# A hybrid decoder layer on one core: modulation in four column groups, two projections half ahead, and a first stage in written order

## The chip, the cores and the metric

The kernel runs on one core of a Trainium2 chip. A core has five engines with queues of their own: TensorE (PE in the profile; its weight loads are PEld), VectorE (DVE), ScalarE (ACT), GpSimd (POOL) and SyncE (SP), which here only issues transfers. Each engine works through its queue in order; semaphores tie the queues together. The metric is the device time of the program in microseconds, as the median of several executions.

## The reference

The reference computes one step of a hybrid decoder layer for a prompt (1024 rows) and eight single rows (the samples), with the same weights. The lines that matter here are those of the projection and of the compression; kv has six kinds (0 to 5), of which the even ones are rotated:

```python
    mod = jax.nn.silu(c) @ p['w_ada'] + p['b_ada']
    shift, scale, gate = jnp.split(mod[:, None, :], 3, axis=-1)
    h = rmsnorm(x, p['g_pre']) * (1 + scale) + shift
    z = h @ p['w_in']
...
    q = rope(zq.reshape(B, T, N_HEADS, HEAD_DIM), pos).reshape(B, T, KV_HEADS, HEADS_PER_GROUP, HEAD_DIM)
    kv = zkv.reshape(B, T, 6, KV_HEADS, HEAD_DIM)
    kv = jnp.stack([rope(kv[:, :, i], pos) if i % 2 == 0 else kv[:, :, i] for i in range(6)], axis=2)
...
    kc = compress(kv[:, :, 0], p['pe_cmp'][0], p['w_cmp1'][0], p['w_cmp2'][0])
    vc = compress(kv[:, :, 1], p['pe_cmp'][1], p['w_cmp1'][1], p['w_cmp2'][1])
```

Behind it come attention in three branches, a gated short convolution, and an output projection with a norm. The condition c has nine rows, one for the prompt and one for each sample.

## The kernel before

Activations stand transposed: model columns on partitions (eight tiles of 128, index k or f), the 1032 rows along the free side in three chunks c of 344 (`CH`). A product in near-fp32 precision is made of three fp32r products: each operand is split into a high part (a rounded copy, on ACT or DVE) and a low part (the difference, on DVE or POOL), and high·high, high·low and low·high are added up. `mm` (line 102), `copy` (lines 106 and 108) and `sub` (line 111) are helpers through which nearly all of that goes, so the lines of the profile are often theirs.

**The first stage** turns x into `Hh` and `Hl`, the split h. For each tile t of 128 rows, `norm_x(t)` squares and sums on ACT (`sq`), makes the mean on DVE (`ss`) and the inverse root on POOL; `scale_x(t)` multiplies on DVE; `trans_x(t)` transposes eight blocks on PE into two banks `psS`, which DVE and ACT copy into `xT`. The modulation has six blocks of 512 columns of `w_ada`; four are needed here: 2 and 3 are the scale for f = 0..3 and 4..7, 0 and 1 the shift. `ada(b)` multiplies the nine condition rows with a block (tiles `ar`, eight of 128 x 512): even k as an fp32 product (`cf`), odd k split into `ah` and `al` with two products (`cA`). `ada_end(b)` copies the sum to `mod`, adds the bias row b_ada that was loaded into its last row, and turns it by four small products with `ksel`; the result becomes `mA` or `mB`. `make_h(f, c)` is one ACT instruction (scale `mA`, bias `mB`) into `htmp`, a cast into `Hh` and a subtraction into `Hl`.

**Weights** of the projections come through the class `Weights`: `load` fetches a piece into one of three buffers `wraw`, `do_split` splits it into `wh` and `wl` (three buffers each), `release` frees one and splits the next. The first pieces are the K/V kinds 0 and 1 (two halves of K each), then q. A projection has 72 products, 24 a chunk.

**Behind the stage** the first projection (kind 0) runs half by half of K, then `proj` does kind 1 and q 0, q 1, with small jobs hung in at given places: `rows_out` and `x_prompt` (of kind 0), and `x_sample`, which needs rows of the paged cache. These are fetched by sixteen indirect transfers on POOL (`gather`, line 417) by the table `idx`, which DVE makes from the page table. `compress1(0)` needs all of them.

**Order.** A scheduler orders each engine's queue from the written program by its own estimates; buffers (`bufs=`) tie transfers and work: four tiles of x, eight `ar`, one `mod`.

Of the kernel before, what the change touches and what calls it, by code (L numbers as in the profile page):

```python
# [39 lines left out]
def constants():  # L40
# [41 lines left out]
def _build(ctx, tc, nc, I, O):  # L82
# [36 lines left out]
    prmT = cst.tile([128, 52], F32, name="prmT")  # L119
# [86 lines left out]
    W.add_cols(kvc(0))  # L206
    W.add_cols(kvc(1))
# [74 lines left out]


    xT = sp.tile([128, KT, TT], F32, name="xT")
    pt = bank("T")
    for k in range(KT):
        PE.transpose(pt[:, k * 9:(k + 1) * 9], ct[:, k * 128:(k + 1) * 128], ident[:9, :9])
    cf = sp.tile([128, KT, 18], F32, name="cf")
    V.memset(cf, 0.0)
    th = sp.tile([128, KT, 9], F32, name="th")  # L290
    cT = pt[:, 0:72].rearrange("p (k c) -> p k c", c=9)
    A.activation(th, cT, AF.Tanh, scale=0.5)
    V.scalar_tensor_tensor(th, th, 1.0, cT, op0=OP.add, op1=OP.mult)
    V.tensor_scalar(cf[:, :, 0:9], th, 0.5, None, op0=OP.mult)
    copy(V, cA[:, :, 0:9], cf[:, :, 0:9])
    sub(V, cA[:, :, 9:18], cf[:, :, 0:9], cA[:, :, 0:9])
# [66 lines left out]
    def make_h(f, c):  # L363
# [11 lines left out]
    load_x(0)
    load_x(1)
    load_x(2)
    load_x(3)
# [1 line left out]
    load_params()  # L380
    load_x(4)
    load_x(5)
    load_x(6)
    load_x(7)
    load_x(8)
# [25 lines left out]
    cache = I["cache_kv_pages"][0]  # L411
    rows2 = cache.rearrange("n p (h k) g d -> (n p h) (k g d)", h=2)

    def gather(out, s, what):

        for par in range(2):
            nc.gpsimd.indirect_dma_start(
                out=out[:, par], out_offset=None, in_=rows2,
                in_offset=bass.IndirectOffsetOnAxis(ap=idx[:, what, s, par:par + 1], axis=0))
# [4 lines left out]
    norm_x(0)  # L424
    scale_x(0)
    trans_x(0)
    norm_x(1)
    scale_x(1)
    trans_x(1)
    norm_x(2)  # L430
    scale_x(2)
    trans_x(2)
    norm_x(3)
    scale_x(3)
    trans_x(3)
    ada(2)
    pt = bank("T")
    PE.transpose(pt[:, 0:52], prm, ident[:52, :52])
    copy(V, prmT, pt[:, 0:52])
    V.tensor_scalar(prmT[:, 8:20], prmT[:, 8:20], 0.5, None, op0=OP.mult)  # L440
    norm_x(4)
    scale_x(4)
    trans_x(4)
    norm_x(5)
    scale_x(5)
    trans_x(5)
    norm_x(6)
    scale_x(6)
    trans_x(6)
    norm_x(7)  # L450
    scale_x(7)
    trans_x(7)
    norm_x(8)
    scale_x(8)
    trans_x(8)
    ada(0)
    scale_done(2, ada_end(2))
    copy(V, mB[:, 0:4, :], ada_end(0))
    make_h(0, 0)
    make_h(1, 0)  # L460
    make_h(2, 0)
    make_h(3, 0)
    W.do_split()
    ada(3)
    W.do_split()
    ada(1)
    make_h(0, 1)
    make_h(1, 1)
    make_h(2, 1)
    make_h(3, 1)  # L470
    make_h(0, 2)
    make_h(1, 2)
    make_h(2, 2)
    make_h(3, 2)
    scale_done(3, ada_end(3))
    copy(V, mB[:, 4:8, :], ada_end(1))
# [938 lines left out]
```

## Time and profile before

| | us |
|---|---|
| median of 3 runs | 1108.38 (1108.06 to 1109.43) |
| profiled execution, own time | 1110.11 |
| its span, first to last instruction | 1108.3 |
| PE busy | 1068.2 |
| DVE busy | 679.4 |
| ACT busy | 458.2 |
| POOL busy | 148.6 |

The profile is of one execution; its time is the span and 1.8 us around it. PE's busy time is nearly the span, but matmul ends are modelled, so stalls are better read from the timeline of a stretch: each row gives the start, the busy time, engine, line, operation, output and inputs, and in brackets the idle time before it with what ended it.

### The profile page before, as it was taken

To read this page: it belongs to the slowest core of one execution; us is meant where nothing else is said; L and a number is where in the kernel's file an instruction comes from. 1 tells how busy PE (TensorE), PEld (TensorE's weight loads), DVE (VectorE), ACT (ScalarE), POOL (GpSimd) and SP (SyncE) were. 2 spreads that over 40 slices of the span, in tenths; PEclk is the share of its full clock that TensorE was granted. 3 is DMA by queue.
4 is the path that set the end of the run, shared out by engine and by line. 5 is a ranking of instruction groups with operands and counts; after the bars stand their busy time and mean duration, and the time that the engine had idled before them with its cause. 6 is when DMAs were issued, how large, how long until landed. Compare 5 with 4: busy or idle time off the path is not lost.

```text
span 1108.3 us, 17275 instructions
## 1 busy us (share of the span) xinstructions
PE 1068.2 (96%) x6406; PEld 970.8 (88%) x6406; DVE 679.4 (61%) x1819; ACT 458.2 (41%) x1025; POOL 148.6 (13%) x190
## 2 busy tenths in 40 slices
PE   6989999999999999999999999999999999999997
PEld 3288999988888899888888999999999999998785
DVE  5865567546988898878987844434356321484433
ACT  5647353446677767776665311111012111121220
POOL 2233000012232111111111510000000000020000
PEclk9889999998999999999999999999999999999999
DMA  9634322310000000000000322362232112242222
GB/s 326 182 80 129 99 74 56 92 40 20 20 20 20 20 20 13 12 16 20 20 20 20 92 65 57 96 190 58 58 96 49 47 43 53 86 124 78 67 87 76
DMA packets 97122, 75.97 MB, mean 69 GB/s; under 512 B 24775, under 2 KB 81270, under 8 KB 97038
## 3 DMA queue, kind: packets, MB, share of 16 engines
q1 hardware_dynamic: 95494, 70.67, 22.6%
q0 software_dynamic: 1536, 4.20, 1.2%
q8 instruction: 50, 0.82, 0.3%
q14 instruction: 34, 0.28, 0.1%
q10 hardware_dynamic: 8, 0.01, 0.0%
HBM read 65.84 MB, written 9.01 MB: 68 GB/s over the span
## 4 chain that ended last, share of the span: by engine, by line
PE 82%; DVE 11%; ACT 3%; DMA 2%; issue 1%; POOL 0%; DVEq 0%; POOLq 0%; SPq 0%; ACTq 0%
PE psacc L102 50%; PE psS L102 17%; PE psO L102 6%; PE psT L987 5%; DVE P L955 3%; DVE P L939 2%; ACT P L942 1%; PE psT L102 1%; PE psS L360 1%; DVE pl L111 1%; DVE pc L111 1%; DVE qh L108 1%; DMA mod<-b_ada 1%; DVE sm L948 1%; DMA ar<-w_ada 1%
## 5 line engine op out<-in xcount | busy, mean ns | idle before, releaser
L102 PE MATMUL psacc<-Hh,wh 128*128 128x344 f32 x1096 | 363.6, 332 | 0.0
L102 PE MATMUL psacc<-Hh,wl 128*128 128x344 f32 x1096 | 352.4, 322 | 0.0
L102 PE MATMUL psacc<-Hl,wh 128*128 128x344 f32 x1096 | 352.2, 322 | 0.0
L102 PEld LDWEIGHTS psacc<-Hh,wh 128*128 128x128 f32 x1096 | 207.5, 189 | 6.1 <-issue 0.4
L102 PEld LDWEIGHTS psacc<-Hl,wh 128*128 128x128 f32 x1096 | 207.6, 189 | 4.5 <-issue 0.4
L102 PEld LDWEIGHTS psacc<-Hh,wl 128*128 128x128 f32 x1096 | 206.9, 189 | 2.2 <-DVE wl L111 0.5
L942 ACT ACTIVATE P<-P,mx 128x64 f32<-128x64 f32 (+8 forms) x192 | 115.0, 600 | 48.4 <-DVE mx L939 47.8
L108 DVE CAST wh<-wraw 128x512 fp32r<-128x512 f32 x78 | 34.1, 442 | 120.3 <-PE psacc L102 114.1
L111 DVE TENSOR_TENSOR pl<-psT,ph 128x512 fp32r<-128x512 f32 x132 | 89.7, 686 | 28.5 <-ACT ph L106 27.9
L111 DVE TENSOR_TENSOR wl<-wraw,wh 128x512 fp32r<-128x512 f32 x114 | 77.9, 687 | 30.1 <-ACT wh L106 25.4
L106 ACT ACTIVATE ph<-psT 128x512 fp32r<-128x512 f32 x132 | 77.5, 591 | 39.5 <-PE psT L987 38.8
L939 DVE CUSTOM_DVE_ANT_0 P<-psS,kbig 128x64 f32<-128x64 f32 (+4 forms) x192 | 81.1, 433 | 11.4 <-PE psS L102 10.5
L987 PE MATMUL psT<-ident,P 128*128 128x128 f32 x528 | 83.8, 277 | 2.7 <-DVE mx L939 1.4
L987 PEld LDWEIGHTS psT<-ident,P 128*128 128x128 f32 x528 | 64.3, 142 | 13.6 <-issue 3.5
L102 PE MATMUL psS<-K,qh 128*128 128x384 f32 (+3 forms) x192 | 66.1, 347 | 2.1 <-DVE mx L939 1.6
L111 POOL TENSOR_TENSOR wl<-wraw,wh 128x512 fp32r<-128x512 f32 x26 | 34.6, 1333 | 224.9 <-ACT wh L106 207.3
L102 PE MATMUL psS<-K,ql 128*128 128x384 f32 (+3 forms) x192 | 63.7, 333 | 0.0
L102 PE MATMUL psO<-pl,V 128*128 128x512 f32 x132 | 60.1, 456 | 1.0 <-DVE pl L111 0.9
L106 ACT ACTIVATE wh<-wraw 128x512 fp32r<-128x512 f32 x62 | 38.8, 627 | 41.4 <-PE psS L102 20.2
L111 POOL TENSOR_TENSOR WOl<-wor,WOh 128x512 fp32r<-128x512 f32 x8 | 11.4, 1419 | 328.4 <-PE psS L102 303.7
L102 PE MATMUL psO<-ph,V 128*128 128x512 f32 x132 | 52.1, 395 | 0.0
L955 DVE TENSOR_SCALAR P<-P,sm 128x640 f32<-128x640 f32 (+7 forms) x104 | 47.2, 512 | 0.7
(346 smaller groups left out, 1839.1 us busy)
## 6 DMA issues: line engine op xcount, KB each, us to landing
wraw<-w_in SPq DMA_DIRECT2D x76, 256.0 KB
ar<-w_ada SPq DMA_DIRECT2D x32, 256.0 KB
x<-x_prompt SPq DMA_DIRECT2D x8, 512.0 KB
wraw<-w_in SPq DMA_DIRECT2D x32, 128.0 KB
wraw<-w_cmp SPq DMA_DIRECT2D x16, 256.0 KB
wraw<-w_ada SPq DMA_DIRECT2D x16, 256.0 KB
wor<-w_out SPq DMA_DIRECT2D x16, 256.0 KB
xr<-x_prompt SPq DMA_DIRECT2D x8, 512.0 KB
```

Source lines behind the costliest of these rows:

```text
L102: PE.matmul(out, lhsT, rhs, start=start, stop=stop, skip_group_check=True)
L106: A.activation(out, in_, AF.Copy)
L108: eng.tensor_copy(out, in_)
L111: eng.tensor_tensor(out=out, in0=a, in1=b, op=OP.subtract)
L360: PE.transpose(pt[:, f * 128:(f + 1) * 128], xs[t][:, (4 * h + f) * 128:(4 * h + f + 1) * 128], ident)
L939: V.tensor_tensor_reduce(out=u.P[:, j, o:o + n], in0=ps[:, :n], in1=m, scale=1.0, scalar=init, op0=OP.add, op1=OP.min, accum_out=u.mx[:, j ...
L942: A.activation(u.P[:, j, 0:u.n], u.P[:, j, 0:u.n], AF.Exp, bias=u.mx[:, j, ci:ci + 1], scale=-1.0, accum_out=u.sm[:, j:j + 1])
L948: V.tensor_tensor(out=u.sm[:, 4:8], in0=u.sm[:, 4:8], in1=gate[:, u.i, 12 * u.g + u.br:12 * u.g + u.br + 10:3], op=OP.mult)
L955: V.tensor_scalar(p, p, u.sm[:, 4 + jj:5 + jj], None, op0=OP.mult)
L987: PE.transpose(pt[:, j * 128:(j + 1) * 128], u.P[:, j, n * 128:(n + 1) * 128], ident)
```

## The change

The modulation is no longer split. `ada` makes eight fp32 products a block, each with 32 columns of `cf` (nine in use) at one of four column positions of the PE array; the four partial sums stand on partitions 0, 32, 64 and 96 of one bank, and the small products of `ada_end` add them up by a constant `ksum` of ones. The bias comes with the parameters (`prm`, now 76 rows, transposed to `prmT`) and is added for each partition in `scale_done` and `shift_done`. The kinds 0 and 1 are projected side by side: the first halves of K of chunks 0 and 1 of both come ahead of blocks 3 and 1, those of chunk 2 around their ends, and the second halves follow the second half of `make_h`; six banks hold the sums. And the whole stage, up to the copies of these two projections, stands in written order on all engines (`manual_schedule`). `ar` has 13 buffers now, `mod` two. The four splits of the first weights have their low parts on POOL, and the index table and the gathers are written behind the last `make_h`.

```diff
-    W.add_cols(kvc(0))
-    W.add_cols(kvc(1))
+    for hf in range(2):
+        for n in range(2):
+            W.add((4, 128), [(lambda t: t, w_in[:, 4 * hf:4 * hf + 4, KV0 + 128 * n:KV0 + 128 * n + 128])])
...
-    XB, AB, HB, MB = 1, 8, 2, 1
+    XB, AB, MB = 1, 13, 2
...
+    in_order = tc.manual_schedule(engines={mybir.EngineType.PE, mybir.EngineType.DVE, mybir.EngineType.Activation,
+                                           mybir.EngineType.Pool, mybir.EngineType.SP})
+    in_order.__enter__()
...
-    def ada(b):
-        ps = bank("acc")
+    def ada(b, tag):
+
+        ps = bank(tag)
         for k in range(KT):
-            r = wraw.pop((b, k))
-            if k % 2 == 0:
-                mm(ps[:18, :], cf[:, k, :], r, k == 0, k == KT - 1)
-                continue
-            h = sp.tile([128, 512], F32R, name="ah", tag="ah", bufs=HB)
-            l = sp.tile([128, 512], F32R, name="al", tag="al", bufs=HB)
-            copy(A, h, r)
-            sub(V, l, r, h)
-            mm(ps[:18, :], cA[:, k, :], h, k == 0, False)
-            mm(ps[:9, :], cA[:, k, 0:9], l, False, k == KT - 1)
-        m = sp.tile([19, 512], F32, name="mod", tag="mod", bufs=MB)
-        A.dma_start(m[18:19, :], I["b_ada"][:, b * 512:(b + 1) * 512])
-        mods[b] = (ps, m)
...
+            o = 32 * (k % 4)
+            PE.matmul(ps[o:o + 32, :], cf[:, k, :], wraw.pop((b, k)), start=k < 4, stop=k >= 4, skip_group_check=True,
+                      tile_position=(0, o))
+        mods[b] = ps
...
-        sub(P if f % 2 and f < 4 else V, Hl[:, f, cs], tmp, Hh[:, f, cs])
...
+        sub(P if f % 3 == 1 else V, Hl[:, f, cs], tmp, Hh[:, f, cs])
...
+    for t in range(4):
+        norm_x(t)
+        if t:
+            scale_x(t - 1)
+            trans_x(t - 1)
+    scale_x(3)
+    trans_x(3)
+    ada(2, "acc")
+    for t in range(4, 9):
+        load_x(t)
+    load_ada(0)
...
+    norm_x(4)
+    mod2 = ada_sum(2)
+    norm_x(5)
+    scale_x(4)
+    trans_x(4)
...
+    for t in range(6, 9):
+        norm_x(t)
+        scale_x(t - 1)
+        trans_x(t - 1)
+    scale_x(8)
+    trans_x(8)
+    ada(0, "acc")
...
+    for c in range(3):
+        for f in range(4):
+            make_h(f, c)
+        if c < 2:
+            half(0, 0, c)
+            half(1, 0, c)
+    ada(3, "T")
+    ada(1, "T")
+    mods3, mods1 = ada_sum(3), ada_sum(1)
+    half(0, 0, 2)
+    W.release()
+    scale_done(4, ada_end(3, mods3))
+    shift_done(4, ada_end(1, mods1))
+    half(1, 0, 2)
+    W.release()
+    for n in range(2):
+        first[n].append(W.get())
+    W.lo = V
+    for c in range(3):
+        for f in range(4, KT):
+            make_h(f, c)
+        if c < 2:
+            half(0, 1, c)
+            half(1, 1, c)
```

Three places in the queues. First ACT before, from its first square on (`sq,ss` are squares with their sums, `xT` copies of transposed tiles, `ah` high parts of the modulation's weights):

```order
L304 ACTIVATE sq,ss<-x 128x1024
L292 ACTIVATE th<-psT 128x72
L304 ACTIVATE sq,ss<-x 128x1024 x3
L106 ACTIVATE xT<-psS 128x4x128 x2
L106 ACTIVATE ah<-ar 128x512 x2
L106 ACTIVATE xT<-psS 128x4x128 x2
```

and ACT of the change at the same place:

```order
L383 ACTIVATE th<-psT 128x72
L300 ACTIVATE sq,ss<-x 128x1024 x2
L110 ACTIVATE xT<-psS 128x4x128
L300 ACTIVATE sq,ss<-x 128x1024
L110 ACTIVATE xT<-psS 128x4x128
L300 ACTIVATE sq,ss<-x 128x1024
L110 ACTIVATE xT<-psS 128x4x128 x2
L300 ACTIVATE sq,ss<-x 128x1024 x2
```

The first four squares stood ahead of all copies; now the third square stands behind the first copy. DVE of the change over the same tiles (`ss` is the mean, `x<-x,ss` the scaling):

```order
L301 TENSOR_SCALAR ss<-ss 128x1 x2
L306 TENSOR_SCALAR x<-x,ss 128x1024
L112 COPY xT<-psS 128x4x128
L301 TENSOR_SCALAR ss<-ss 128x1
L306 TENSOR_SCALAR x<-x,ss 128x1024
L112 COPY xT<-psS 128x4x128
L301 TENSOR_SCALAR ss<-ss 128x1
L306 TENSOR_SCALAR x<-x,ss 128x1024
```

Each scaling stands behind the mean of the next tile; before, the second mean stood behind the first scaling. Last, DVE before and of the change at the index table (`ptf`, `pif`, `idx`), around the last `make_h`:

```order
L108 CAST Hh<-htmp 128x344
L108 CAST ptf<-pti 128x8
L108 CAST Hh<-htmp 128x344
L406 TENSOR_SCALAR ptf<-ptf,kbig 128x8
L111 TENSOR_TENSOR Hl<-htmp,Hh 128x344
L409 TENSOR_SCALAR pif<-ptf 128x8 x4
L111 TENSOR_TENSOR Hl<-htmp,Hh 128x344
L108 CAST idx<-pif 128x32
L108 CAST Hh<-htmp 128x344
```

```order
L365 TENSOR_TENSOR htmp<-htmp,mB 128x8
L112 CAST Hh<-htmp 128x344
L112 CAST ptf<-pti 128x8
L486 TENSOR_SCALAR ptf<-ptf,kbig 128x8
L489 TENSOR_SCALAR pif<-ptf 128x8 x4
L112 CAST idx<-pif 128x32
L508 STREAM_SHUFFLE pr<-kvraw 128x344
```

The table stood among the `make_h` of the second half, with more of them behind it; now it stands behind the last one, ahead of the first rope (`pr`).

## Rows read from the trace of the kernel before

**Rows 1.** The page: busy time, share of the span and instructions.

```profile
PE 1068.2 (96%) x6406; PEld 970.8 (88%) x6406; DVE 679.4 (61%) x1819; ACT 458.2 (41%) x1025; POOL 148.6 (13%) x190
```

**Rows 2.** Chain of waits, 85 to 120 us: start, us, what.

```profile
91.41 2.68 DMA x<-cache_kv_pages,idx
...
101.62 5.67 PE psacc L102 x36
...
118.19 1.93 PE psS L102 x11
```

**Rows 3.** Timeline of DVE: start, busy us, what, idle before and its releaser.

```profile
6.33 0.15 DVE L305 TENSOR_SCALAR ss<-ss 128x1 f32<-128x1 f32 x1 [5.03 <-ACT sq L304]
...
7.16 0.75 DVE L310 TENSOR_SCALAR x<-x,ss 128x1024 f32<-128x1024 f32 x1 [0.48 <-POOL ss L306]
...
20.52 0.68 DVE L108 COPY mod<-psacc 18x512 f32<-18x512 f32 x1 [1.94 <-PE psacc L102]
...
22.24 0.75 DVE L310 TENSOR_SCALAR x<-x,ss 128x1024 f32<-128x1024 f32 x1 [0.66 <-POOL ss L306]
...
28.68 0.74 DVE L310 TENSOR_SCALAR x<-x,ss 128x1024 f32<-128x1024 f32 x1
...
42.20 0.52 DVE L111 TENSOR_TENSOR Hl<-htmp,Hh 128x344 fp32r<-128x344 f32 x1
...
43.33 1.11 DVE L111 TENSOR_TENSOR Hl<-htmp,Hh 128x344 fp32r<-128x344 f32 x1
```

**Rows 4.** Timeline of ACT.

```profile
5.15 1.06 ACT L304 ACTIVATE sq<-x 128x1024 bf16<-128x1024 f32 x1 [2.60 <-DMA x<-x_prompt]
...
6.49 1.06 ACT L304 ACTIVATE sq<-x 128x1024 bf16<-128x1024 f32 x1
...
27.22 0.60 ACT L106 ACTIVATE xT<-psS 128x512 f32<-128x512 f32 x1 [1.09 <-PE psS L360]
...
41.12 1.80 ACT L368 ACTIVATE htmp<-xT,mB,mA 128x344 f32<-128x344 f32 x3 [2.88 <-DVE mB L108]
...
65.95 3.17 ACT L368 ACTIVATE htmp<-xT,mB,mA 128x344 f32<-128x344 f32 x5 [10.15 <-DVE mB L108]
...
95.69 0.89 ACT L106 ACTIVATE G<-x 128x128 f32<-128x128 f32 x4
```

**Rows 5.** Timeline of POOL: the first and the last of sixteen gathers.

```profile
73.35 1.19 POOL L417 DMA_INDIRECT x<-cache_kv_pages,idx  x1 [14.80 <-DVE htmp L371]
...
93.95 0.94 POOL L417 DMA_INDIRECT x<-cache_kv_pages,idx  x1 [0.30 <-issue]
```

**Rows 6.** Two stretches: us, busy time by engine, PE clock, DMA share, GB/s.

```profile
25.00:30.00 5.00, 4.79 (x18) 3.42 (x18) 3.04 (x8) 3.83 (x8) 1.54 (x3) 0.50 0.53 153
...
90.00:100.00 10.00, 7.87 (x53) 7.35 (x52) 4.26 (x9) 8.86 (x20) 3.82 (x4) 1.00 0.46 139
```

**Rows 7.** Timeline of PE.

```profile
7.97 3.67 PE L360 MATMUL psS<-ident,x 128*128 128x128 f32 x16 [3.85 <-DVE x L310]
...
15.83 1.03 PE L102 MATMUL psacc<-ar,cf 128*18 128x512 f32 x2
16.79 0.40 PE L102 MATMUL psacc<-ah,cA 128*18 128x512 f32 x1
...
20.09 0.39 PE L102 MATMUL psacc<-al,cA 128*9 128x512 f32 x1
...
23.14 1.32 PE L360 MATMUL psS<-ident,x 128*128 128x128 f32 x8 [2.46 <-DVE ss L305]
25.21 3.68 PE L360 MATMUL psS<-ident,x 128*128 128x128 f32 x16 [0.75 <-DVE ss L305]
...
56.52 1.05 PE L102 MATMUL psT<-ksel,mod 19*128 19x9 f32 x8
...
64.25 1.43 PE L102 MATMUL psT<-ksel,mod 19*128 19x9 f32 x8 [3.80 <-DMA mod<-b_ada]
```

**Rows 8.** Timeline of SP's queue: the first transfers of x.

```profile
1.48 1.78 SPq L87 DMA_DIRECT2D x<-x_prompt  x4
```

More of the change, by code (lines that the diff above doesn't have):

```diff
@@ L68, in constants @@
         sel[[s, s + 8], 145 + s] = 1
+    sum4 = np.zeros((128, 9), np.float32)
+    for q in range(4):
+        for i in range(9):
+            sum4[32 * q + i, i] = 1
     pm = (np.arange(128) % 64).astype(np.float32)[:, None]
@@ L118, in _build @@
     msk, cmsk, pmod = kbig[:, 0:768], kbig[:, 768:888], kbig[:, 888:889]
-    prmT = cst.tile([128, 52], F32, name="prmT")
+    prmT = cst.tile([128, 76], F32, name="prmT")
     cA = cst.tile([128, KT, 18], F32R, name="cA")
@@ L281, in load_params @@
         dma(prm[20:52, :], I["pe_cmp"][0].rearrange("k (a c) b -> (k a) (c b)", c=2))
[L284 to L296, printed above, removed]
+        dma(prm[52:76, :], I["b_ada"][0].rearrange("(a b) -> a b", b=128))
+        dma(ksum, I["k_sum"])
     rs = {}
@@ L372, in make_h, with gather @@
         copy(V, Hh[:, f, cs], tmp)
-        sub(P if f % 2 and f < 4 else V, Hl[:, f, cs], tmp, Hh[:, f, cs])
[L375 to L378, printed above, removed]
-    load_ada(2)
[L380 to L385, printed above, removed]
+        sub(P if f % 3 == 1 else V, Hl[:, f, cs], tmp, Hh[:, f, cs])
+    for t in range(4):
+        load_x(t)
+    load_params()
+    load_ada(2)
+    xT = sp.tile([128, KT, TT], F32, name="xT")
+    pt = bank("T")
+    for k in range(KT):
+        PE.transpose(pt[:, k * 9:(k + 1) * 9], ct[:, k * 128:(k + 1) * 128], ident[:9, :9])
+    cf = sp.tile([128, KT, 32], F32, name="cf")
+    V.memset(cf, 0.0)
+    th = sp.tile([128, KT, 9], F32, name="th")
+    cT = pt[:, 0:72].rearrange("p (k c) -> p k c", c=9)
+    A.activation(th, cT, AF.Tanh, scale=0.5)
+    V.scalar_tensor_tensor(th, th, 1.0, cT, op0=OP.add, op1=OP.mult)
+    V.tensor_scalar(cf[:, :, 0:9], th, 0.5, None, op0=OP.mult)
+    copy(V, cA[:, :, 0:9], cf[:, :, 0:9])
+    sub(V, cA[:, :, 9:18], cf[:, :, 0:9], cA[:, :, 0:9])
+    cache = I["cache_kv_pages"][0]
+    rows2 = cache.rearrange("n p (h k) g d -> (n p h) (k g d)", h=2)
+    def gather(out, s, what):
+        for par in range(2):
+            nc.gpsimd.indirect_dma_start(
+                out=out[:, par], out_offset=None, in_=rows2,
+                in_offset=bass.IndirectOffsetOnAxis(ap=idx[:, what, s, par:par + 1], axis=0))
+    for t in range(4):
+        norm_x(t)
[6 more added lines that the diff above has]
+    for t in range(4, 9):
+        load_x(t)
     load_ada(0)
@@ L396, in _build, with half @@
     dma(kbig, I["k_big"])
+    norm_x(4)
[3 more added lines that the diff above has]
+    trans_x(4)
+    pt = bank("T")
+    PE.transpose(pt[:, 0:76], prm, ident[:76, :76])
+    copy(V, prmT, pt[:, 0:76])
+    V.tensor_scalar(prmT[:, 8:20], prmT[:, 8:20], 0.5, None, op0=OP.mult)
+    scale_done(0, ada_end(2, mod2))
+    for t in range(6, 9):
[5 more added lines that the diff above has]
+    ada(0, "acc")
+    W.lo = P
+    W.do_split()
+    W.do_split()
+    shift_done(0, ada_end(0))
+    accs = [[bank("acc"), bank("acc"), bank("S")], [bank("S"), bank("S"), bank("O")]]
+    first = [[W.get()], [W.get()]]
+    def half(n, hf, c):
+        wh, wl = first[n][hf]
+        o, cs = accs[n][c][:, :CH], slice(c * CH, c * CH + CH)
+        for k in range(4 * hf, 4 * hf + 4):
+            mm(o, wh[:, k % 4, :], Hh[:, k, cs], k == 0, False)
+            mm(o, wh[:, k % 4, :], Hl[:, k, cs], False, False)
+            mm(o, wl[:, k % 4, :], Hh[:, k, cs], False, k == KT - 1)
+    for c in range(3):
[22 more added lines that the diff above has]
+            half(1, 1, c)
     pti = rp.tile([128, NS], I32, name="pti")
@@ L410, in _build @@
     copy(V, idx, pif)
[L411 to L419, printed above, removed]
     sct = sp.tile([128, D], F32, name="x", tag="x", bufs=XB)[0:16, 0:512]
     dma(sct, I["state_conv"][0].rearrange("s j c -> (s j) c"))
[L424 to L476, printed above, removed]
-    make_h(4, 0)
-    make_h(5, 0)
-    make_h(6, 0)
-    make_h(7, 0)
-    W.do_split()
-    make_h(4, 1)
-    make_h(5, 1)
-    make_h(6, 1)
-    make_h(7, 1)
-    make_h(4, 2)
-    make_h(5, 2)
-    make_h(6, 2)
-    make_h(7, 2)
     def start_end():
```

60 lines of the change are left out of this document (30 added, 30 removed).

## Prediction

> **What bounds the kernel now.** I read the page first: TensorE (PE) is busy for 1068.2 us, 96% of the span [rows 1]. From about 118 us on it hardly waits, so the time is PE's work plus what the first stage loses, and the change touches only that stage. Behind the first compression, PE's rows and those of the other engines are the same in both programs, so I compare one moment: the start of that compression, 118.2 us in the chain of waits [rows 2]. Whatever moves it moves the end.
>
> Then I followed the timelines of the stage. Three waits set it. First, tiles of x: scale on VectorE (DVE), eight transposes on PE, copies on DVE and ScalarE (ACT). The scalings of tiles 4 to 7 lie 2.15 us apart (22.24 to 28.68, three intervals [rows 3]). The first `make_h` starts at 41.12, when the modulation of block 0 is finished [rows 4]. Second, blocks 3 and 1, interleaved with the first twelve `make_h`; PE then waits for b_ada (3.80 us ahead of 64.25, in the rows of PE below), and `make_h` of the second half starts at 65.95 [rows 4]. Third, the sixteen gathers on GpSimd (POOL): first at 73.35, last at 93.95, 1.37 apart [rows 5]; between 90 and 100 us PE is busy for only 7.87 of 10 [rows 6].
>
> **The change: tiles of x.** In written order ACT squares tile t+1 only after its copy of tile t-1, and DVE scales tile t only after the statistics (`ss`) of tile t+1. That closes a loop: scaling to first transpose 0.81 (7.16 [rows 3] to 7.97 [rows 7]); eight transposes until ACT's copy 2.01 (25.21 [rows 7] to 27.22 [rows 4]); that copy 0.60; square to `ss` 1.18 (5.15 [rows 4] to 6.33 [rows 3]); `ss` 0.15. The sum is 4.75; neighbours on one engine overlap by about a tenth, so 4.6 us a tile. The 2.01 is at half clock (25 to 30 us: 0.50 [rows 6]); sixteen transposes take 3.67 also at 7.97, while eight at 23.14 take 1.32 [rows 7]. PE would work for less than half of each turn, less than around 25 us, so I take the low level. At the high one a turn is 0.7 shorter.
>
> The first scaling waits for the second square, which starts at 6.49 or a little before [rows 4]: 7.8, then 12.4 and 17.0. The fourth needs no square: 17.0 + 0.8 + four transposes 1.2 + copy 0.6 = 19.6, its transposes end at 22.2. Before, ada(2) ends at 20.5 (20.09 + 0.39 [rows 7]).
>
> **The modulation.** Removed for each of four blocks: four splits on ACT and DVE, four fp32 products, and four pairs of products of parts. An fp32 product of 512 columns is two matmul records, 0.96 us (15.83 to 16.79 [rows 7]). Now there are eight a block, in four column groups. No row shows such products. One after another they take 7.7 us; if four run side by side, two rounds, 1.9. I take the value between: the second record of a product needs the columns of the first and can't overlap it, while the next product's first record can, so about nine steps of 0.48, 4.0 after overlap. That is little less than eight products do now.
>
> The Trainium skill, "TensorEngine Tiling" (Key Properties), says that different tiles load weights and multiply in parallel. "TensorE: Matmul & The Clock Gate" (Part 3) gives 2.38 times for three column tiles; an estimate from it is 7.7 / 2.38 = 3.2 us a block. By the first sentence the sum would go by 1.9 (the second rival).
>
> ada(2) starts partly at half clock: 22.2 + 4.5 = 26.7. The copy `mod` (0.68, 20.52 [rows 3]) and a short `ss` stand before the scaling of tile 4, 27.5. Then 4.1 to tile 5 (PE still at full clock; the parameters' transpose, four sum products at 1.05 for eight records [rows 7], and `mA` take as long as ACT's copy and square), 4.6 each to tiles 6 and 7: 31.6, 36.2, 40.8. Tile 8 is scaled at 43.4, transposed by 44.8. ada(0) takes 5.0 (one more for the clock): 49.8. Copy 0.7, sums 1.1, bias 0.25: first `make_h` at **51.9**, before 41.1.
>
> Loads don't decide this. x tiles 6 and 7 can only be issued once transposes free their buffers, at about 19.5 and 22.3, and would need some 4 us (tile 0: issued at 1.48 [rows 8], squared at 5.15 [rows 4]); they are scaled much later. The bias rides in the parameter transfer, so the 3.80 us for which PE waited at 64.25 [rows 7] goes; cover: the parameters are wanted some 20 us after their issue.
>
> **From there to the second half.** A chunk of four `make_h` costs DVE about 2.9 us: four casts, three subtractions of 0.52, and 0.59 for the one on POOL (a subtraction took 1.11 while POOL ran one [rows 3]). The two first halves of chunks 0 and 1 are 48 products of 0.158 (5.67 us for 36 [rows 2]), 7.6 us, paced by `make_h` and half warm: ended 10.2 after the start, 62.1. PE then does ada(3) and ada(1), 8.0, to 70.1. The last three loads of block 1 wait for buffers of block 3 and land near 68.7, when they are wanted at 4.0 a block; with quicker products PE would wait some 2 us for them. One half 1.9, eight sum products 2.1, `mA` and `mB`: **74.4** against 65.95. W.release's splits lie beside this.
>
> **Second half, gathers.** DVE needs 3.1 us a chunk with two subtractions on POOL, in all 10.7: 85.1. The indices are now computed behind the last `make_h`, and POOL issues the gathers behind its last subtraction: first at **86.5** (before 73.35), last 20.6 later; 0.95 and 0.30 to issue, 2.68 to land ([rows 5], [rows 2]): 111.05. PE asks for them in the last transposes of x_sample in the first q projection; everything behind waits. PE's own work would bring it there about 15 us after 85.1 (2.9 for the last halves, 60 products, 25 transposes), and ACT's queue, some 35 copies (four of the smallest take 0.89 [rows 4]), in about 23. So the gathers end last: copies 0.9, transposes 0.6, 112.5. Left are 84 products (13.3), nine transposes (1.0; eight take 1.32 with their tail, 23.14 [rows 7]) and 1.4 for a clock that falls in the wait: **128.2**, 10.0 later.
>
> In the profiled execution 1110.1 (span 1108.3 and 1.8 around it) becomes 1120.1; the runs' median lies 1.7 below it, at 1108.4, hence **1118.4**.
>
> **The rivals.**
> *One after another.* Column groups give nothing: 3.7 more in ada(2) and in ada(0), 7.4 in the pair, so 14.8 more: 1133. For it: no row shows two products at once. Chance 0.12.
>
> *Side by side.* 1.9 a block: 2.1 less in each of ada(2) and ada(0), 4.2 in the pair less some 2 for the late loads, 6 in all: 1112. Chance 0.26. The skill's sentence on tiles that run in parallel is this rival; no row here shows it.
>
> *The tiles of x don't run as a loop (not slower).* If something in my loop does not hold, tiles follow each other as now, 2.15 apart: 5.3 less before the fourth, 6.9 less between the fifth and the eighth, 12.2 in all: 1106. It decides from a period of 2.9 us down, which takes away 10. For it: DMA moves tiles fast enough, and each engine's own work a tile is below 2.2. Against it: both queues are in order, and each of the loop's steps has its row. Chance 0.14.
>
> *The gathers don't end last.* Were they quicker (below 1.1 us each), ACT would end last 4.3 earlier: 1114. For it: DVE is idle then. Against it: 1.37 also after DVE slackened. Chance 0.06, the sum otherwise as forecast.
>
> **How the numbers follow.** The forecast itself has 0.42, with its own range 1113 to 1124: one tile period more or less, and the gathers' hand-over. 0.2% is 2.2 us, about what a measurement of this kernel can tell. Faster: two thirds of the loop rival, some of the side-by-side one: 0.15. Within: 0.08. Slower: 0.77. For 8 in 10 the range leaves out most of the one-after-another case and the far end of the loop rival: 1103 to 1130.
>
> **What would show it.** The scalings of x tiles 4.6 us apart, with PE near half clock; first `make_h` at 52, second-half one at 74, first gather at 86, compression at 128; eight column products from first start to last end in 4 us; no wait for b_ada; PE idle for several us before the x_sample transposes. I am wrong if x tiles come 3 us apart or less, if a block takes 2 us and the compression starts before 118, or if PE does not wait for gathers.

## The result, and the profile after

The changed kernel takes 1116.25 us (median of 6 runs, 1114.8 to 1117.5), the kernel before in the same comparison 1109.26 (1108.06 to 1112.25): a ratio of 1.0058, 95% interval 1.0043 to 1.0074. It is slower by 0.6%. The profiled execution took 1116.27, with a span of 1114.5.

The head of its page, against [rows 1]: PE is busy 9 us less and the span is 6.2 us longer, so the loss is waiting, not work.

```profile
span 1114.5 us, 17207 instructions
...
PE 1059.0 (95%) x6406; PEld 973.6 (87%) x6406; DVE 671.7 (60%) x1792; ACT 449.3 (40%) x1009; POOL 158.0 (14%) x197
```

**The tiles of x.** DVE's timeline of the start (start, busy time, engine, line, operation), against [rows 3]. The scalings stand at 8.33, 12.89 and 17.45 and, from tile 5 on, 4.62 apart, twice the 2.15 of before; the loop is there, and PE's clock is at half over it, as forecast (0.50 from 30 to 40 us, the first window in the next block of rows).

```profile
8.33 0.75 DVE L306 TENSOR_SCALAR x<-x,ss 128x1024 f32<-128x1024 f32 x1
...
12.89 0.75 DVE L306 TENSOR_SCALAR x<-x,ss 128x1024 f32<-128x1024 f32 x1
...
17.45 0.75 DVE L306 TENSOR_SCALAR x<-x,ss 128x1024 f32<-128x1024 f32 x1
...
30.99 0.75 DVE L306 TENSOR_SCALAR x<-x,ss 128x1024 f32<-128x1024 f32 x1
...
35.61 0.75 DVE L306 TENSOR_SCALAR x<-x,ss 128x1024 f32<-128x1024 f32 x1
...
40.23 0.75 DVE L306 TENSOR_SCALAR x<-x,ss 128x1024 f32<-128x1024 f32 x1
...
88.89 0.17 DVE L112 CAST ptf<-pti 128x8 f32<-128x8 int32 x1 [1.00 <-DMA pti<-page_table]
...
89.79 0.18 DVE L112 CAST idx<-pif 128x32 int32<-128x32 f32 x1
```

**The blocks.** PE's rows of the products with w_ada, against [rows 7] (two records a product), and the windows beside them (columns: PE busy with its records, PEld, DVE, ACT, POOL, PE's granted clock, DMA share, GB/s). Block 0 takes 3.64 us at half clock (1.2 GHz). Block 2 took 3.59; the profile's record of the clock begins only at 26.3 us, where block 2 ends, so that its level is read from its pace. The row of 26 records holds block 3 and five products of block 1, 3.62 us at the full 2.4 GHz; then the last three products, each released by its load, last until 69.4, while the transfers run at 311 GB/s.

```profile
44.60 3.64 PE L315 MATMUL psacc<-ar,cf 128*32 128x512 f32 x16
...
62.62 3.62 PE L315 MATMUL psT<-ar,cf 128*32 128x512 f32 x26
66.41 3.00 PE L315 MATMUL psT<-ar,cf 128*32 128x512 f32 x6 [0.17 <-DMA ar<-w_ada]
...
30.00:40.00 10.00, 4.29 (x18) 3.45 (x18) 3.45 (x8) 4.01 (x8) 2.02 (x2) 0.50 0.74 248
...
62.00:65.00 3.00, 3.00 (x29) 1.19 (x28) 2.06 (x7) 0.00 (x0) 0.00 (x0) 1.00 0.10 11
65.00:69.00 4.00, 3.78 (x12) 0.52 (x7) 0.38 (x1) 0.00 (x0) 0.00 (x0) 1.00 1.01 311
```

**From there to the compression.** The chain of waits (start, duration, who), against [rows 2] and [rows 5]. Block 3 alone is 1.98 us. The weights of the second halves come late, then the page table is on the chain for 10.70 us, then sixteen gathers from 90.27 on, and the first compression starts at 130.31, before at 118.19.

```profile
62.69 1.98 PE psT L315 x16
68.27 5.95 DMA wraw<-w_in
...
78.10 10.70 DMA pti<-page_table
90.27 1.16 POOL x L395
...
110.60 2.77 DMA x<-cache_kv_pages,idx
...
130.31 4.74 PE psS L106 x27
```

PE stood waiting ahead of the last transposes of gathered rows, as forecast: 1.78 us here, 1.01 a few rows earlier.

```profile
109.26 0.44 PE L617 MATMUL psS<-ident,G 128*128 128x128 f32 x2 [1.01 <-ACT G L110]
...
114.02 0.55 PE L617 MATMUL psS<-ident,G 128*128 128x128 f32 x3 [1.78 <-ACT G L110]
```

So the stage lost 12.1 us and the span only 6.2. The table follows both executions by the first record of a tile (us from the span's start; `qh`, by its first record on DVE, begins attention, `csr` stands behind it, `GG` ahead of the gates, `sq` of the output projection ahead of the tail), with some of the later runs.

| kernel | first `make_h` | compression | qh | csr | GG | sq | span |
|---|---|---|---|---|---|---|---|
| before | 41.1 | 118.0 | 244.2 | 659.4 | 825.9 | 1014.5 | 1108.3 |
| after | 51.3 | 130.1 | 256.2 | 668.3 | 834.8 | 1023.2 | 1114.5 |
| e1 | 38.1 | 114.5 | 240.6 | 655.0 | 821.5 | 1010.0 | 1101.2 |
| e2 | 50.3 | 121.9 | 248.0 | 660.4 | 826.8 | 1015.3 | 1106.5 |
| e7 | 40.4 | 120.1 | 246.1 | 660.8 | 827.3 | 1015.8 | 1107.3 |
| e8 | 49.7 | 127.7 | 253.7 | 666.6 | 833.2 | 1021.8 | 1115.2 |

Compression to qh, csr to GG and GG to sq are alike to 0.2 us in all. Two stretches are not: by unrounded times, qh to csr took 415.1 before and 412.2 after (3.0 less), sq to the end 93.8 and 91.2 (2.6 less). 12.1 less 5.6 and some tenths is 6.2.

The 12.1 is a difference of two single traces. The runs e7 and e8 have the instructions of before and after at other addresses, and their compressions lie 7.6 us apart (120.1 and 127.7), their spans 7.9. So what the stage loses is known to a few us only.

### The profile page after: what moved, and what is told of

Its sections match the earlier page's. It is cut to its first block, busy times and chain, and to the rows that moved or that the text cites. A ratio compares the mean times of both kernels' runs of the same rounds, so it can differ in the third digit from the quotient of the medians.

```text
span 1114.5 us, 17207 instructions
## 1 busy us (share of the span) xinstructions
PE 1059.0 (95%) x6406; PEld 973.6 (87%) x6406; DVE 671.7 (60%) x1792; ACT 449.3 (40%) x1009; POOL 158.0 (14%) x197
## 4 chain that ended last, share of the span: by engine, by line
PE 79%; DVE 11%; ACT 4%; DMA 2%; issue 2%; POOL 2%; SPq 0%; DVEq 0%; POOLq 0%; ACTq 0%
PE psacc L106 46%; PE psS L106 17%; PE psO L106 6%; PE psT L984 4%; DVE P L952 3%; DVE P L936 2%; POOL x L395 1%; ACT P L939 1%; PE psS L354 1%; PE psT L106 1%; DMA pti<-page_table 1%; DVE pl L115 1%; DVE qh L112 1%; DVE pc L115 1%; PE psacc L315 1%
## 5 line engine op out<-in xcount | busy, mean ns | idle before, releaser
L106 PE MATMUL psacc<-Hh,wh 128*128 128x344 f32 x1072 | 357.6, 334 | 2.8 <-DVE Hh L112 2.8
L106 PE MATMUL psacc<-Hl,wh 128*128 128x344 f32 x1072 | 347.0, 324 | 0.7 <-POOL Hl L115 0.6
L106 PE MATMUL psacc<-Hh,wl 128*128 128x344 f32 x1072 | 346.9, 324 | 0.0
L106 PEld LDWEIGHTS psacc<-Hh,wh 128*128 128x128 f32 x1072 | 204.7, 191 | 9.1 <-DVE Hh L112 3.1
L106 PEld LDWEIGHTS psacc<-Hl,wh 128*128 128x128 f32 x1072 | 204.6, 191 | 6.0 <-POOL Hl L115 1.4
L106 PEld LDWEIGHTS psacc<-Hh,wl 128*128 128x128 f32 x1072 | 204.0, 190 | 2.4 <-DVE wl L115 0.5
L115 DVE TENSOR_TENSOR wl<-wraw,wh 128x512 fp32r<-128x512 f32 x110 | 75.1, 687 | 33.3 <-ACT wh L110 28.6
L110 ACT ACTIVATE ph<-psT 128x512 fp32r<-128x512 f32 x132 | 77.3, 590 | 36.5 <-PE psT L984 36.0
L936 DVE CUSTOM_DVE_ANT_0 P<-psS,kbig 128x64 f32<-128x64 f32 (+4 forms) x192 | 81.2, 434 | 10.6 <-PE psS L106 9.7
L115 POOL TENSOR_TENSOR wl<-wraw,wh 128x512 fp32r<-128x512 f32 x30 | 39.6, 1323 | 235.0 <-ACT wh L110 234.3
L952 DVE TENSOR_SCALAR P<-P,sm 128x640 f32<-128x640 f32 (+7 forms) x104 | 47.3, 513 | 0.7
```

The lines of the kernel that those rows point to most:

```text
L106: PE.matmul(out, lhsT, rhs, start=start, stop=stop, skip_group_check=True)
L110: A.activation(out, in_, AF.Copy)
L115: eng.tensor_tensor(out=out, in0=a, in1=b, op=OP.subtract)
L936: V.tensor_tensor_reduce(out=u.P[:, j, o:o + n], in0=ps[:, :n], in1=m, scale=1.0, scalar=init, op0=OP.add, op1=OP.min, accum_out=u.mx[:, j ...
L952: V.tensor_scalar(p, p, u.sm[:, 4 + jj:5 + jj], None, op0=OP.mult)
```

## The experiments

Experiments that ran together share their runs of the kernel before, so ratios go by those: it took 1109.8 (e1, e2, e4, e6), 1109.1 (e3, e5, e7, e8), 1128.3 (e9 to e11) and 1131.0 (e12).

**e1_x_tiles: the squares and scalings a tile ahead.**

```diff
-    for t in range(4):
-        norm_x(t)
-        if t:
-            scale_x(t - 1)
-            trans_x(t - 1)
-    scale_x(3)
-    trans_x(3)
+    norm_x(0)
+    scale_x(0)
+    norm_x(1)
+    for t in range(4):
+        if t < 2:
+            norm_x(t + 2)
+        if t < 3:
+            scale_x(t + 1)
+        trans_x(t)
...
```

Tiles 4 to 8 follow in the same way.

> The changed kernel, with only the order of the x tiles altered: ACT squares tile t+2 and DVE scales tile t+1 before tile t is transposed, so that the loop scaling, transposes, copy, square, scaling has a tile in hand. Theory (the written order closes a loop over one tile, 4.6 us a turn): scalings 2.2 to 2.6 us apart, first make_h near 40 to 41 instead of 51.3, first gather and first compression earlier by 8 to 10.5. For the end: 1106 to 1108 if what the changed kernel regained behind 130 us does not depend on the delay, about 1111 if half of any delay is regained there. Rival (something else spaces the tiles, loads or the low TensorE clock): scalings still 3.5 us or more apart, first make_h at 47 or later, the time within 3 us of 1116.

Measured: 1100.89 us, ratio 0.9924 (0.9905 to 0.9942): 15 us below the changed kernel, and below the kernel before. DVE's scalings of tiles 4 to 7 and GpSimd's first gather:

```profile
20.93 0.75 DVE L306 TENSOR_SCALAR x<-x,ss 128x1024 f32<-128x1024 f32 x1
...
22.75 0.75 DVE L306 TENSOR_SCALAR x<-x,ss 128x1024 f32<-128x1024 f32 x1
...
24.76 0.74 DVE L306 TENSOR_SCALAR x<-x,ss 128x1024 f32<-128x1024 f32 x1
...
27.73 0.75 DVE L306 TENSOR_SCALAR x<-x,ss 128x1024 f32<-128x1024 f32 x1
...
76.22 1.16 POOL L395 DMA_INDIRECT x<-cache_kv_pages,idx  x1 [1.40 <-DVE idx L112]
```

They lie 2.27 apart on average, the first `make_h` is at 38.1 (13 earlier), the gathers start 14 earlier and the compression 15.6. The theory holds, with a larger gain than expected, and the time lies below both of its figures; the rival falls. Behind the compression 2.3 us of the gain were given back, all between qh and csr.

**e2_gathers: page table, indices and gathers ahead of block 0.**

```diff
     W.load()
     W.load()
+    dma(kbig, I["k_big"])
+    for j in range(2):
+        src = I["page_table"]
+        dma(pti[64 * j:64 * j + 64, :], bass.AP(tensor=src.tensor, offset=src.offset + j, ap=[[0, 64], [2, NS]]))
     load_ada(3)
...
     trans_x(8)
+    copy(V, ptf, pti)
...
+    copy(V, idx, pif)
...
+            gather(g[:, i], s + i, 0)
...
     ada(0, "acc")
-    W.lo = P
...
-        sub(P if f % 3 == 1 else V, Hl[:, f, cs], tmp, Hh[:, f, cs])
+        sub(P if f in (4, 7) else V, Hl[:, f, cs], tmp, Hh[:, f, cs])
```

> The changed kernel, with the page table loaded before block 3, and indices and all gathers issued ahead of the product of block 0; GpSimd's subtractions of the first half are given to VectorE, since GpSimd is then busy with the gathers. Theory (late gathers hold PE at the last transposes of the sample values): the first gather near 45 us instead of 90.3, the last landed before 75, no wait of PE for G near 114, and the first compression 4 to 6 us earlier than 130.3 (what is left is ACT's queue of copies); end 1111 to 1113. Rival (ACT or PE would be as late without the gathers): the compression less than 1.5 us earlier, 1115 to 1117.

Measured: 1108.54 us, ratio 0.9985 (0.9971 to 0.9998). The gathers go out from 47.3 to 66.7, PE's waits for G shrink to 0.23 and 0.50 us, and the compression comes at 121.9, 8.2 earlier. The theory holds and was too small. The gain is not the gathers' alone: e2 also takes subtractions off GpSimd and the index work off the end of the stage, and its first `make_h` is 1.0 us earlier.

**e4_one_group: eight products on the same columns.**

```diff
-            PE.matmul(ps[o:o + 32, :], cf[:, k, :], wraw.pop((b, k)), start=k < 4, stop=k >= 4, skip_group_check=True,
-                      tile_position=(0, o))
+            mm(ps[0:32, :], cf[:, k, :], wraw.pop((b, k)), k == 0, k == KT - 1)
```

> The changed kernel, with its eight fp32 products of a block all on the first 32 columns instead of four column groups, accumulated one after another; the sum product reads 32 rows. Everything else is as changed. Theory (the groups run side by side, a block takes 2.0 us at the full clock and 3.6 at half): a block takes 7.7 us at the full clock (0.96 a product), and up to 15 at half; blocks 2 and 0 together 8 to 20 us later, the pair of blocks 3 and 1 about 10 us longer; time 1132 to 1145. Rival (what spaces the products is their loads and weights, not the groups): a block 4 us or less, time 1116 to 1122.

Measured: 1132.68 us, ratio 1.0207 (1.0187 to 1.0227), 16.4 above the changed kernel. PE's rows of blocks 2, 0, and 3 with 1:

```profile
22.35 8.99 PE L106 MATMUL psacc<-ar,cf 128*32 128x512 f32 x16
...
49.39 9.12 PE L106 MATMUL psacc<-ar,cf 128*32 128x512 f32 x16
...
72.27 13.92 PE L106 MATMUL psT<-ar,cf 128*32 128x512 f32 x32
...
49.40:53.40 4.00, 4.00 (x6) 0.88 (x6) 0.22 (x1) 0.13 (x1) 2.17 (x2) 0.50 0.24 63
54.00:58.40 4.40, 4.40 (x11) 0.99 (x9) 0.00 (x0) 0.00 (x0) 0.00 (x0) 1.00 0.78 228
```

The pair's sixteen products take 13.92 us at the full clock, 6.96 a block against 1.98; blocks 2 and 0 take 9.0 and 9.1 instead of 3.6. The groups do run side by side. The rival falls with them, and so does the forecast's rival of products one after another. The time is at the lower end of what was expected, since neither block 2 nor block 0 ran at half clock throughout: the two windows (columns as for the blocks of the changed kernel) show block 0 at 0.50 and then at 1.00, and block 2's records are 0.86 us apart until 26.4 us and 0.43 from there.

**e6_modulation: the kernel before with the new modulation alone** (column groups, bias with the parameters, thirteen `ar`; order, projections and gathers as before; `ada` and `ada_end` as in the change's diff).

> The kernel before, with only the new modulation: fp32 products in four column groups, bias per partition out of the parameter transfer, thirteen buffers for the rows of w_ada; the order of work, the first projection and the gathers stay as before. Theory (the groups and the bias save PE time, the written order and the late gathers lose it): a block 2.0 us at the full clock, no wait of 3.8 us for b_ada near 64 us, make_h of the second half 3 to 6 us before 65.95; the first compression 2 to 5 us before 118.2; time 1104 to 1108. Rival (the stage is bound by x tiles, make_h on VectorE and the gathers, not by the modulation): compression within 1.5 us of 118.2, time 1108 to 1111.

Measured: 1102.56 us, ratio 0.9939 (0.9922 to 0.9956). So the modulation by itself makes the kernel faster, and the rest of the change makes the whole slower. Where it gains is less clear: the profiled execution took 1106.62, the longest of its six, and its compression starts at 117.8, hardly earlier, with PE waiting 2.35 us for ACT near 85 us in place of the wait for b_ada. 2.5 us are the tail's (e7).

**e3_both: e1 and e2 together.**

> The order of the x tiles of e1_x_tiles and the early page table and gathers of e2_gathers together, all else as changed. Theory (two losses in a row on the path: the loop of tiles, 15 us by its run, and the gathers that PE and ACT wait for, 8 us by its run; in e1 the gathers still went out from 76 to 97 us): both together remove more than the larger alone, the first compression at 106 to 110 us, the time 1093 to 1097. Rival (one cover hides both: with the tiles in a row, VectorE, ACT or the loads of w_ada bind): compression at 112 us or later, the time 1099 to 1102.

Measured: 1103.02 us, ratio 0.9945 (0.9925 to 0.9964): slower than e1. The theory falls; the rival has the compression (119.1), and the time lies 1 us above its range. DVE, ahead of the indices, and the window beside it:

```profile
39.76 0.17 DVE L112 CAST ptf<-pti 128x8 f32<-128x8 int32 x1 [10.00 <-DMA pti<-page_table]
...
30.00:40.00 10.00, 1.35 (x16) 0.14 (x6) 0.21 (x2) 0.36 (x1) 0.00 (x0) 0.68 0.35 95
```

DVE stood 10.0 us for the page table, and block 0's sum behind it; first `make_h` at 44.8. Later PE waited 2.3 us for block 1's loads beside the gathers (the 7 us that the expectations below name were DVE's wait for PE's sum).

**e5_scheduler: the changed kernel in the scheduler's order** (the three lines of `in_order` left out).

> The changed kernel without its five in-order engine queues: the same program, but the scheduler orders the first stage as it orders the rest. Theory (what loses the time is the written order, not what is computed in it): scalings of x tiles about 2.2 us apart, first make_h between 36 and 42 us, the first compression between 114 and 121 us, time 1101 to 1108. Rival (the new work itself, the first half of two projection tiles ahead of blocks 3 and 1, delays the second half): first make_h early, but the compression at 126 us or later, time above 1112.

Measured: 1110.97 us, ratio 1.0015 (1.0000 to 1.0030). Scalings and first `make_h` (35.3) are as the theory has it, the compression (124.2) and the time lie between theory and rival. What was overlooked is again the page table, issued at 72.8 us behind seven loads of weights (in the changed kernel at 77.3, behind as many); DVE's row, and PE's for the state rows that stand behind it in the same queue:

```profile
84.83 0.17 DVE L112 CAST ptf<-pti 128x8 f32<-128x8 int32 x1 [8.77 <-DMA pti<-page_table]
...
85.19 0.57 PE L494 MATMUL psT<-ident,x 16*128 16x16 f32 x4 [7.28 <-DMA x<-state_conv]
```

**e7_shift_before and e8_shift_after: nothing but addresses.**

```diff
-    prmT = cst.tile([128, 52], F32, name="prmT")
+    prmT = cst.tile([128, 76], F32, name="prmT")[:, 0:52]
```

and in the changed kernel 84 columns of which 76 are used.

> The kernel before, with the tile of the transposed parameters 76 columns wide instead of 52, of which 52 are used: no instruction differs, but all tiles behind it in the left half of SBUF lie 96 bytes further on. It asks where the 2.5 us come from that every kernel with the new parameters gained between the first product of the output projection and the end (before: 93.8 us from the first sq to the span's end; changed and four variants: 91.2 to 91.3; products of 512 columns start 0.233 us apart before, 0.227 after). Theory (the addresses of the weights of that projection set the pace): 0.227 us apart, 91.3 us, the time 2.5 us below before, 1106 to 1107.5. Rival (something else of the old modulation, such as the second DMA queue that ACT used, lasts until the end): 0.233 us apart, 93.8 us, time as before within 1 us.

> The changed kernel, with the tile of the transposed parameters 84 columns wide instead of 76, of which 76 are used: no instruction differs, but all tiles behind it in the left half of SBUF lie 32 bytes further on (128 bytes further than before). Theory (the addresses set the pace of the output projection, and a shift by 128 bytes is like none): products 0.233 us apart there, the time 2.5 us above the changed kernel, 1118 to 1119.5. Rival (addresses don't matter, or only the distance of 96 bytes from before does not): 0.227 us apart, 1115 to 1117.

Measured: e7 1106.82 us, ratio 0.9978 (0.9963 to 0.9992), 2.2 below; e8 1117.64, ratio 1.0080 (1.0061 to 1.0100), 1.4 above the changed kernel and just below the theory's range. PE's rows of the output projection, the first and the eleventh product from 1049.7 us on, of e7:

```profile
1049.77 0.39 PE L102 MATMUL psS<-WOl,mh 128*128 128x512 f32 x1
...
1052.04 0.39 PE L102 MATMUL psS<-WOh,ml 128*128 128x512 f32 x1
```

and of e8:

```profile
1049.75 0.40 PE L106 MATMUL psacc<-WOh,ml 128*128 128x512 f32 x1
...
1052.08 0.40 PE L106 MATMUL psS<-WOh,mh 128*128 128x512 f32 x1
```

Ten products take 2.27 us in e7 and 2.33 in e8; in the kernel before they took 2.33, in the changed one 2.27. The whole output projection, from its first product to its last, takes 96.8 us in before and e8 and 94.3 in after and e7. From sq to the end it is 91.6 in e7 and 93.4 in e8. The theory holds in both directions: the wider parameter tile moved what lies behind it by 96 bytes, and with that the pace of the output projection. In e8's time the tail's loss shows less than full, since its compression came 2.4 us earlier in the profiled execution, with the same instructions.

**e9_table_early: the mask tile and the page table loaded ahead of block 3, all else in place** (the first part of e2's diff).

> The changed kernel, with only the loads of the mask tile and the page table moved ahead of the loads of block 3; indices and gathers stay behind the last make_h. In every trace so far the load of the page table takes about 11 us from issue to landing (10.70 in the changed kernel), also when little else is moving, and in the changed kernel it is issued at 77.3. Theory (the gathers began 3.8 us later than predicted because of this load alone): the first gather at 86 to 87.5 us instead of 90.3, PE's waits and the first compression 3 to 4 us earlier, time 1112 to 1114. Rival (GpSimd's last subtractions hold the gathers just as long): the first gather at 89 or later, time 1115 to 1117.

Measured: 1123.68 us, ratio 0.9954 (0.9939 to 0.9969). GpSimd's last subtraction, its first gather, and a row of ACT later:

```profile
87.03 0.91 POOL L115 TENSOR_TENSOR Hl<-htmp,Hh 128x344 fp32r<-128x344 f32 x1 [3.10 <-DVE ptf L112]
88.91 1.16 POOL L395 DMA_INDIRECT x<-cache_kv_pages,idx  x1 [0.97 <-DVE idx L112]
...
111.28 0.60 ACT L110 ACTIVATE X<-psS 128x512 fp32r<-128x512 f32 x1 [5.46 <-remote]
```

DVE no longer waits for the table, but the first gather is only 1.4 us earlier: the load was 1.0 us of the 3.8, and theory and rival were both off, the rival less. What follows can't be read: ACT stands 5.46 us ahead of 111.28 with no releaser but "remote" (more of this under e10 to e12), and the compression comes at 132.0. The time was inconclusive.

**e10_between, e11_table_first and e12_between_again.** e10 has e1's tiles, e2's early loads, and the indices and gathers between the two halves of `make_h`; e11 is e3 with page table and row numbers loaded with the parameters; e12 is e10 again.

```diff
+    W.lo = V
+    copy(V, ptf, pti)
...
+    copy(V, idx, pif)
...
+            gather(g[:, i], s + i, 0)
...
     ada(3, "T")
     ada(1, "T")
...
-        sub(P if f % 3 == 1 else V, Hl[:, f, cs], tmp, Hh[:, f, cs])
+        sub(P if f == 1 else V, Hl[:, f, cs], tmp, Hh[:, f, cs])
```

> The order of the x tiles of e1_x_tiles; mask tile and page table loaded ahead of block 3; indices and gathers between the two halves of make_h, on a GpSimd that has nothing else to do then (its subtractions of the second half and the splits of the weights go to VectorE). Theory (in e1 the gathers still ended last, and in e3 it was the early place of indices and gathers, ahead of block 0, that cost: VectorE waited 10.0 us for the page table, PE 7 us for loads of w_ada beside the gathers): no wait for G or the page table, first make_h at 38, compression at 108 to 112 us, time 1095 to 1098.5. Rival (the gathers delay the loads of block 1 here too, or ACT's queue of copies ends as late as the gathers did): compression at 113.5 us or later, time 1100 to 1103.

> e3_both, with the page table and the column of row numbers out of the mask tile loaded with the parameters at the start, so that VectorE does not wait for them ahead of block 0; gathers still ahead of block 0. Theory (of e3's loss against e1, the wait for the page table is one part, the gathers' transfers beside those of w_ada the other): first make_h at 37 to 39 us instead of 44.8, PE waits some 5 to 9 us for the loads of block 1 near 50 us, compression at 112 to 116 us, time 1098 to 1101.5. Rival (the wait for the page table was all of the loss): compression at 108 to 111 us, time 1094 to 1097.

> The kernel of e10_between once more, on whatever chip this call has: e9 to e11 ran where the kernel before took 1128 us instead of 1109, with a stretch between 610 and 680 us that was some 6 us longer than in all traces before it. Theory (that stretch belongs to that chip or moment, and the kernel's own gain is the 3.9 us that its first compression starts ahead of that of e1): compression at 110 to 111.5 us, the stretch 56 to 57 us from the last mx to csr, time 12 to 15 us below before (1095 to 1098 where before takes 1109). Rival (the longer stretch belongs to this kernel's order): 62 us or more there again, time 1102 or above.

Measured: e10 1108.07 us, ratio 0.9828 (0.9804 to 0.9852); e11 1120.69, 0.9927 (0.9909 to 0.9945); e12 1113.38, 0.9856 (0.9822 to 0.9890). e10's compression starts at 110.6, 3.9 ahead of e1's, as the theory has it, e12's at 113.9, which its theory misses. The rest of the time does not follow: in e10 and e12 PE stands still while gathers are being issued, with no releaser in the profile ("issue"). In e12:

```profile
67.57 0.66 PE L106 MATMUL psacc<-Hh,wh 128*128 128x344 f32 x1 [7.32 <-issue]
...
631.92 0.65 PE L106 MATMUL psacc<-Hh,wh 128*128 128x344 f32 x1 [6.39 <-issue]
```

Waits of that kind, on PE, DVE or ACT and of 0.7 to 8.9 us, stand in all four traces of e9 to e12, during or right after both sets of gathers, and in none of the ten others; the second set belongs to attention and is the same in all kernels. The stretch around it, from the last mx to csr, took 62.4 to 64.7 us in these four, whatever their order, and 56.1 to 57.0 in the others. So e12's rival has the stretch, but it is not this order that makes it. The kernel before took 19 to 22 us more beside e9 to e12 as well, which points to the chip or the moment; the record gives e12 the same chip number as e3, e5, e7 and e8, beside which the kernel before took 1109.1, so, if the number names one chip, a chip that is always slow does not explain it. No trace of the kernel before from that time shows where its time went, and the cause stays open. Whether e10 beats e1 stays open. e11 was wrong in both theories: its page table, issued from 10.0 us on and landed at 23.3, held up everything behind it. The window:

```profile
10.00:20.00 10.00, 4.63 (x27) 3.42 (x25) 4.75 (x9) 3.42 (x6) 2.02 (x2) 0.95 0.04 1
20.00:30.00 10.00, 5.90 (x16) 1.45 (x16) 0.00 (x0) 0.00 (x0) 0.00 (x0) 0.53 0.89 333
```

Eight loads of w_ada were issued from 11.4 us on, and from 10 to 20 us 1 GB/s moved; first `make_h` at 48.5.

## Why the prediction was right, and where it was not

**The loop of tiles: right.** A period of 4.6 and a first `make_h` at 51.9 were forecast; 4.56 to 4.62 and 51.3 came. e1 shows that this order is the larger loss: without it 15.4 us go, more than the whole slowdown.

**"4.0 after overlap": mis-sized.** The step that let each next product overlap only the first record of the one before it was wrong. At the full clock a block takes 1.98 us, as in the side-by-side rival; e4 shows 6.96 without groups, 3.5 times as much. It did little harm because blocks 2 (by its pace) and 0 ran at half clock, 3.6 each where 4.5 and 5.0 were put, and because the pair of blocks then lost 2.8 us to the last three loads, about as that rival said (2): 6.8 in place of 8.0, where 4.0 would have done. The Trainium skill's sentence in "TensorEngine Tiling (Array Packing)" (Key Properties), that different tiles load weights and multiply in parallel, agrees with the 1.98 us against e4's 6.96. The 2.38 times that the Trainium skill gives for three column tiles in "TensorE: Matmul & The Clock Gate" (Part 3) gave an estimate of 3.2 us; for four, the runs show 3.5 times.

**The bias: right.** No engine waits for b_ada any more.

**From the second half to the gathers: 3.8 us short.** A chunk of four `make_h` was put too low already in the first half: DVE's first two chunks there took 3.3 each, not 2.9, and the pieces that the prediction lists come to 3.5 with a cast's 0.34. The second half began at 74.8 (74.4 forecast). "In all 10.7" for its three chunks became 12.7: the last cast into `Hh` starts at 87.55. Of these the first two took 3.4 us of DVE each, the third 5.6, as it holds eight small products for the sample rows, which the sum left out; beside a subtraction on POOL such a product took 0.93 instead of 0.17.

```profile
82.50 0.93 DVE L365 TENSOR_TENSOR htmp<-htmp,mB 128x8 f32<-128x8 f32 x1
...
87.28 0.17 DVE L365 TENSOR_TENSOR htmp<-htmp,mB 128x8 f32<-128x8 f32 x1
```

Then DVE waited 1.0 us for the page table and needed 1.1 for the indices, so the first gather went out at 90.27, not 86.5. The load's own 10.7 us had no place in the sum; it was hidden in the kernel before, where it was issued at 53.8.

**PE waits for the gathers: right, and worth more than thought.** The rival without these waits had 4.3 us; e2 gained 8.2 at the compression, with the index work and subtractions moved as well.

**"Whatever moves it moves the end": the step that failed.** The compression came 12.1 us later (10.0 forecast), the end 6.2. Two things make up 5.5 of the 5.9, and the prediction had neither:
- 2.5 us: the wider `prmT` shifts what lies behind it by 96 bytes, and the products of 512 columns start 0.227 us apart instead of 0.233. Shown by e7 and e8. Which operand's address it is was not tried.
- 3.0 us: in attention PE's clock fell to half for shorter times. Lined up product by product, the changed kernel gains 1.3 us on the one before between 248 and 257 us (times of before) and 1.5 between 594 and 601, the two places where the clock fell in before. The rows of before there:

```profile
249.00:256.00 7.00, 6.63 (x28) 6.05 (x28) 4.89 (x26) 4.08 (x18) 2.38 (x5) 0.51 0.01 2
597.00:601.00 4.00, 3.91 (x16) 3.65 (x17) 3.40 (x13) 2.25 (x5) 0.92 (x1) 0.57 0.23 63
```

and of after, at the same two places of the program:

```profile
261.00:266.00 5.00, 4.63 (x22) 4.12 (x22) 3.50 (x18) 3.32 (x14) 1.84 (x5) 0.66 0.01 2
609.00:613.00 4.00, 4.00 (x30) 3.88 (x29) 4.00 (x14) 3.91 (x8) 0.93 (x1) 1.00 0.00 0
```

What is missing from the full clock is 7 x 0.49 = 3.4 us and 4 x 0.43 = 1.7 before, 5 x 0.34 = 1.7 and nothing after: 3.4 us in all, enough for the 3.0. At the second place the runs bear this out: the clock falls there in before, e1, e6 and e7 (qh to csr 414.4 to 415.1) and not in after, e2, e3, e4, e5 and e8 (412.2 to 413.0). At the first it is argued only: e3, e4, e5 and e8 have a dip as long as that of before and yet gain 0.7 to 0.9 us there. PE waits for DVE ahead of the second dip in all of them; why the clock falls in some and not in others was not found.

In e7 and e8 the same step would have passed for right (7.6 at the compression, 7.9 at the end), since there the fast output projection is on the side of before, and qh to csr still gives 1.7 back.

That the time came out near the forecast (1116.25 for 1118.4) is partly luck. The stage ended 2.1 us later than forecast, 5.9 us were given back behind it and not counted, and 1.7 us were taken off for the median although the changed kernel's median lies at the time of its profiled execution; but for 2.1 us these errors offset each other. The side, faster or slower, was right for the reason given: with either of the two named losses taken away, the loop (e1) or the late gathers (e2), the kernel is no longer slower than the one before.

## What to carry to other kernels

When a queue gets a written order, follow one tile through all engines' queues and ask whether an instruction of the next tile stands behind the last one of this tile; one tile of lead turned a loss of 7 us into a gain of 9 (2.5 of it by addresses). A change that resizes any tile also moves every address behind it: run the old kernel with the new size before crediting the change with what happens far from it. And look at when a small scattered load is issued, not only at how many bytes it has: behind the page table's 4 KB the queue moved 1 GB/s in e11.

## What the runs showed of the hardware that was not expected

- The page table, two transfers of 64 x 8 single integers (4 KB in all), lands 10.6 to 11.2 us after the issue of the second in eight of the traces and 12.6 to 14.5 in the six that load it earlier (e2, e3, e9 to e12), and holds up the queue behind it: 1 GB/s in e11's window, 7.28 us of PE's wait in e5.
- The same products on the same engine run 3% slower or faster by the place of their tiles in SBUF: 0.233 or 0.227 us a product, at a granted clock of 1.00.
- Eight fp32 products in four column groups take 1.98 us at 2.4 GHz and 3.6 at 1.2 GHz; on one column group they take 6.96 at 2.4 GHz.
- With the same instructions at other addresses, the first compression starts at 118.0 or 120.1 (before, e7) and at 130.1 or 127.7 (after, e8), and the same program gave 110.6 and 113.9 (e10, e12): in single traces a milestone of this stage moved by 2 to 3.3 us.
- In four traces (e9 to e12) PE, DVE or ACT stood still for up to 8.9 us while gathers were being issued or right after, released by nothing that the profile shows; in ten others none did.
